# Low parts of the input projections' weights: an adding transfer onto the negated high parts in place of a VectorE subtraction

## The chip, the cores and the metric

The kernel runs on one core of one Trainium2 chip. The metric is the device time of one execution in microseconds (us). The kernel before took 2382.75 us as the median of 3 runs (2381.59 to 2386.46). The execution whose profile is read here took 2386.67 us; its trace spans 2384.9 us.

The engines are named as the profile names them: PE is TensorE (PEld its weight loads), DVE is VectorE, ACT is ScalarE, POOL is GpSimd, SP is SyncE. Each runs its own instructions strictly in the order in which they were recorded.

## The reference

The reference is a trunk of two layers on 1024 tokens of width 1024, in float32. Each layer is a mixer and then a convolutional feed-forward network (FFN), each between two RMS norms:

```python
for l in range(DEPTH):
    h = rms_norm(x, norm_mix_pre[l])
    proj = h @ w_in[l]                       # 1024 x 3072, twelve slices of 256 columns
    (c_a, c_gate, sb_q, sb_k, sb_v, r_q, r_k, r_v, r_g,
     sc_b, sc_c, sc_h) = jnp.split(proj, N_IN_SLICES, axis=-1)
    y_conf = conformer_conv(c_a, c_gate, ...)             # depthwise convolution of 31 taps
    y_sb = merge_heads(stick_breaking_attention(...))     # 4 heads, blocks of 128 queries
    y_ret = retention_mixer(r_q, r_k, r_v, r_g, ...)      # chunks of 128 tokens
    y_sc = short_gated_conv(sc_b, sc_c, sc_h, ...)        # 3 taps
    mix = jnp.concatenate([y_conf, y_sb, y_ret, y_sc], axis=-1) @ w_out[l]
    x = x + rms_norm(mix, norm_mix_post[l])
    f = conv_ffn(rms_norm(x, norm_ffn_pre[l]), ffn_up[l], ffn_conv_w[l], ffn_down[l])
    x = x + rms_norm(f, norm_ffn_post[l])
```

## The kernel before, in words

**Split products.** Every matrix product is done with both operands split into a high part (the value rounded to the type that PE multiplies) and a low part (what the rounding left). One product is three matmuls: high by high, high by low, low by high. For the input projection `hH` and `hL` are the parts of the normed tokens, kept in place, and `wh` and `wl` those of the weights.

**Weights of the input projection.** The 3072 columns of `w_in` are 24 weights of 1024 x 128 a layer. `load_weight` (L188 to L196) makes each one ready: SP issues the load of 512 KB into `wr`, of which there is one buffer; ACT casts it to `wh` (L193); the engine that is named in the queue, here always DVE, subtracts `wh` from `wr` into `wl` (L195). There are two buffers of `wh` and two of `wl`, so a weight can be made ready while PE works with the one before; PE frees the pair of the weight before that by its last matmul. `wr` is free for the next load when the last engine that reads it has done so.

**Projection.** `project` (L214) runs 48 matmuls of 128 x 512 for a weight (L210), in eight steps of six: two with `wh` and `hH`, two with `wh` and `hL`, two with `wl` and `hH`. The first matmul that needs `wl` is therefore the fifth. The first two weights of a layer are done together in `project_pair`.

**What runs between.** From the third weight on, PE's order is written out by hand (`manual_schedule`). Between two of the eight steps `run_slot` sets the other work of the mixer at slots of a fixed table. Three pieces of it matter here.

- Stick-breaking attention, in units: PE makes scores (L361, L362, L364) in one fixed bank of PSUM; ACT takes |z|, exp and log (L371 to L373); DVE combines (L375) and scans (L379); ACT takes an exp (L381); PE transposes (L396), ACT and DVE split the result (L181, L182), PE multiplies by the values (L409), and ACT and DVE (L416 to L418) add the parts. The next unit's scores wait until the scan has read the bank.
- Retention: PE makes products within chunks (L494) and outputs (L513, L518) in PSUM banks that it takes over from projections and from earlier steps; DVE must have drained these first (L182, L329, L379, L522, L523). Its norm takes a mean, a square and a variance (L530, L538 on PE; L541 and L542 on ACT; L543 and L546 on DVE). Its queries and keys are rotated on DVE (L437 to L439), with a swap of partitions by DMA between.
- The depthwise convolution: 30 taps for each of two halves, each tap one DVE instruction over about 1024 columns (L261). Taps have the lowest priority: the scheduler, which orders DVE, ACT, SP and POOL by its own estimates of time and by priorities, puts them wherever it thinks that DVE would be free.

**After the projections** come the output projection (its weights go through the same `wr`, L613), a boundary with the norms, and the FFN. In the FFN and for the first weights of a layer nothing is changed here.

Of the kernel before, what the change touches and what calls it, by code (L numbers as in the profile page):

```python
# [7 lines left out]
F32 = mybir.dt.float32  # L8
F32R = mybir.dt.float32r
AF = mybir.ActivationFunctionType  # L10
ALU = mybir.AluOpType
# [56 lines left out]
OTHER = (0, 2, 4)  # L68
HPR = 1000
HPW = 0  # L70
WPOOL = []
UPOOL = ()
SKEW = 0
NPLAIN = 3
# [12 lines left out]
def trunk_kernel(ctx, tc, x, w_in, w_out, w_up, w_down, params, gains, consts, rope, out):  # L87
    nc = tc.nc
# [32 lines left out]
    def ufree(*ts):  # L121
        for t in ts:
            free.append(slot_of.pop(id(t))[0])
# [60 lines left out]
    def gain(i):  # L184
        g = ualloc()
        nc.sync.dma_start(g, gains[i].partition_broadcast(P))
        return g

    def load_weight(src, eng):
        raw = wp.tile([P, KT, P], F32, tag="wr", name="wr", bufs=WR)  # L190
        nc.sync.dma_start(raw, src)
        wh = wp.tile([P, KT, P], F32R, tag="wh", name="wh")
        nc.scalar.copy(wh, raw)  # L193
        wl = wp.tile([P, KT, P], F32R, tag="wl", name="wl")
        eng.tensor_sub(wl, raw, wh.bitcast(F32))  # L195
        return wh, wl  # L196

    queue = []
    ready = []

    def prefetch(n=1):
        while queue and len(ready) < n:
            with tc.high_priority(offset=HPW):
                ready.append(load_weight(*queue.pop(0)))
# [345 lines left out]

    psum("pp")
    nc.scalar.preload_act_table_set("natural_log_exp_and_others")
    queue += [(w_in[0, n], nc.gpsimd if n in WPOOL else nc.vector) for n in range(24)]
    hhs = []
    for t in range(NB + SKEW):
        if t == XP:
# [22 lines left out]
    for l in range(DEPTH):  # L579
# [409 lines left out]
        def down_tok(gs, ws, t, first, final):  # L989
            ps = ptile(t % FB if final else nextp())  # L990
            down_mm(ps, gs, ws, t, range(2))
            if first:
                facc[t] = ualloc()
                with tc.high_priority(offset=HPE):
                    nc.vector.tensor_copy(facc[t], ps)
            else:
                nc.vector.tensor_add(facc[t], facc[t], ps)  # L997
            if final:
                boundary(t, facc[t], ps, g_post, g_pre, xin, xs[2 * l + 1] if g_pre is not None else out, XF[t])

        def down_end(gs, ws, t):

            rows = slice(t * P, (t + 1) * P)
            f, ps, xt = facc[t], ptile(t % FB), ualloc()
            nc.sync.dma_start(xt, xin[rows, :])
            tt = ualloc()
            ss = []
            for half in range(2):
                hs = slice(half * 512, (half + 1) * 512)
                down_mm(ps, gs, ws, t, (half,))  # L1010
                nc.vector.tensor_add(f[:, hs], f[:, hs], ps[:, hs])
                ss.append(square_sum(f[:, hs], ps[:, hs]))
                nc.vector.tensor_mul(tt[:, hs], f[:, hs], g_post[:, hs])
            nc.vector.tensor_add(ss[1], ss[0], ss[1])
            r = rstd_of(ss[1])
            for half in range(2):
                hs = slice(half * 512, (half + 1) * 512)
                nc.vector.scalar_tensor_tensor(tt[:, hs], tt[:, hs], r, xt[:, hs], ALU.mult, ALU.add)
                nc.sync.dma_start(out[rows, hs], tt[:, hs])
            ufree(xt, tt, f)  # L1020

        def down_load(j, where):

            w = down_split(w_down[l, j * P:(j + 1) * P, :], where)
            g = down_split(gd[j], None if where is None else where + 1)
            return g, w
# [37 lines left out]
        for ci, ch in enumerate(chunks):  # L1064
            final = ci == len(chunks) - 1
            if final:
                if not last:
                    queue += [(w_in[l + 1, n], nc.gpsimd if n in WPOOL else nc.vector) for n in range(24)]
                    prefetch(2)
                g_post, g_pre = gain(4 * l + 3), None if last else gain(4 * l + 4)  # L1070
            pairs = [loads[j] for j in ch]
            gs, ws = [p[0] for p in pairs], [p[1] for p in pairs]
            for t in range(NB):
                if final and last and t == NB - 1:
                    down_end(gs, ws, t)
                else:
                    down_tok(gs, ws, t, ci == 0, final)
                if t in (0, 1) and ci and todo and not final:
                    j, where = todo.pop(0)
                    loads[j] = down_load(j, where)  # L1080
            if places[ci] is None:
                for g, w in zip(gs, ws):
                    ufree(*g, *w)
            if ci == 0:
                for _ in range(4):
                    j, where = todo.pop(0)
                    loads[j] = down_load(j, where)
# [74 lines left out]
```

## Time and profile before

| | |
|---|---|
| median of 3 runs | 2382.75 us |
| the profiled execution | 2386.67 us |
| its span | 2384.9 us |
| PE busy | 2297.3 us (96%) |
| DVE busy | 1674.2 us (70%) |
| ACT busy | 1080.7 us (45%) |
| POOL busy | 196.5 us (8%) |

The page and the answers of the trace give times from the start of the span. Layer 0's mixer with its projections lies at about 25 to 430 us, layer 1's at about 1210 to 1640 us; the FFNs lie between and behind. A row of the timeline gives start, length, engine, line and operation, what it writes and reads, how many instructions are in the row, and in brackets how long the engine was idle before it and who released it.

### The profile page before, as it was taken

What the parts mean: (1) busy time and instruction counts of PE and PEld (TensorE: products, weight loads), DVE (VectorE), ACT (ScalarE), POOL (GpSimd) and SP (SyncE); (2) the same over time, 40 slices, a digit from 0 to 9 for tenths busy, and PEclk for the clock granted to TensorE, in tenths of its full rate; (3) what the DMA queues carried; (4) which work ended last, traced back from release to release, by engine and by line L of the source; (5) the groups of instructions that cost most, each with busy time, mean ns of one, the idle gap of its engine ahead of it and who ended that gap; (6) DMA issues with size and microseconds to landing.
All of it is one profiled execution on the core that took longest, in us unless ns stands there. A gap on an engine that the chain in (4) does not pass through costs nothing.

```text
span 2384.9 us, 26334 instructions
## 1 busy us (share of the span) xinstructions
PE 2297.3 (96%) x10596; PEld 1885.0 (79%) x10596; DVE 1674.2 (70%) x1749; ACT 1080.7 (45%) x1463; POOL 196.5 (8%) x84
## 2 busy tenths in 40 slices
PE   7998999999999999999999989999999999999998
PEld 6876787787888888788778767877888888888886
DVE  4699877559777777644556998775598777774445
ACT  5663565434455445421246535654344554453112
POOL 0000000000000000643210000000000000016420
PEclk9998999999999999999999989999999999999999
DMA  4212212412122224522222122123122222235223
GB/s 150 71 53 63 62 36 88 138 48 92 68 88 89 80 80 143 183 80 98 80 80 71 53 62 62 36 95 135 53 89 80 80 80 89 87 121 176 84 71 124
DMA packets 58810, 209.87 MB, mean 88 GB/s; under 512 B 7104, under 2 KB 7872, under 8 KB 58688
## 3 DMA queue, kind: packets, MB, share of 16 engines
q1 hardware_dynamic: 58688, 208.19, 26.7%
q8 instruction: 83, 1.36, 0.2%
q14 instruction: 39, 0.32, 0.0%
HBM read 159.93 MB, written 39.85 MB: 84 GB/s over the span
## 4 chain that ended last, share of the span: by engine, by line
PE 38%; DVE 7%; ACT 3%; DMA 1%; issue 1%; DVEq 0%; SPq 0%
PE pp L984 10%; PE pp L210 9%; PE ppx L901 8%; PE ppy L901 4%; DVE u L261 2%; PE ppz L901 2%; PE pp L738 1%; DVE u L182 1%; ACT u L151 1%; DMA wr<-in_w_out 1%; PE op L409 1%; DVE u L379 1%; DVE u L167 1%; PE tp L396 0%; DMA wr<-in_w_up 0%
## 5 line engine op out<-in xcount | busy, mean ns | idle before, releaser
L261 DVE SCALAR_TENSOR_TENSOR u<-u,par,u 128x1023 f32<-128x1023 f32 (+10 forms) x280 | 356.3, 1284 | 28.6 <-ACT u L793 24.4
L210 PE MATMUL pp<-hH,wh 128*128 128x512 f32 x960 | 327.2, 411 | 1.0 <-DVE u L182 0.5
L997 DVE TENSOR_TENSOR u<-u,pp 128x1024 f32<-128x1024 f32 x143 | 174.6, 1221 | 209.9 <-PE pp L984 209.8
L210 PE MATMUL pp<-hL,wh 128*128 128x512 f32 x960 | 312.7, 396 | 0.0
L210 PE MATMUL pp<-hH,wl 128*128 128x512 f32 x960 | 311.5, 395 | 0.0
L984 PE MATMUL pp<-u,u 128*128 128x512 f32 x1152 | 266.0, 392 | 6.1 <-ACT u L955 4.6
L984 PEld LDWEIGHTS pp<-u,u 128*128 128x128 f32 x1152 | 216.6, 189 | 52.4 <-ACT u L955 5.4
L974 POOL TENSOR_TENSOR hH<-u,hH 128x1024 fp32r<-128x1024 f32 x24 | 58.1, 2451 | 1946.5 <-ACT hH L973 1946.5
L210 PEld LDWEIGHTS pp<-hL,wh 128*128 128x128 f32 x960 | 183.6, 191 | 40.4
L210 PEld LDWEIGHTS pp<-hH,wl 128*128 128x128 f32 x960 | 183.2, 191 | 40.3
L210 PEld LDWEIGHTS pp<-hH,wh 128*128 128x128 f32 x960 | 172.6, 193 | 37.5 <-issue 5.9
L738 PE MATMUL pp<-u,hH 128*128 128x512 f32 x512 | 140.2, 392 | 0.4 <-ACT u L181 0.4
L984 PE MATMUL pp<-hH 128*128 128x512 f32 x576 | 131.5, 389 | 0.0
L984 PEld LDWEIGHTS pp<-hH 128*128 128x128 f32 x576 | 108.1, 188 | 22.4
L901 PE MATMUL ppx<-u,wh 128*128 128x512 f32 x384 | 118.4, 389 | 0.3 <-ACT u L926 0.3
L793 ACT ACTIVATE u<-u,par 128x1024 f32<-128x1024 f32 x76 | 87.8, 1156 | 67.4 <-DVE u L947 65.6
L738 PEld LDWEIGHTS pp<-u,hH 128*128 128x128 f32 x512 | 95.0, 188 | 20.4 <-ACT u L181 1.2
L195 DVE TENSOR_TENSOR wl<-wr,wh 128x1024 fp32r<-128x1024 f32 x60 | 73.3, 1221 | 50.9 <-ACT wh L193 50.7
L973 ACT CAST u<-u 128x1024 fp32r<-128x1024 f32 x48 | 50.2, 1052 | 128.9 <-DMA u<-in_w_down 85.7
L901 PE MATMUL ppx<-u,hH 128*128 128x512 f32 x352 | 108.4, 389 | 0.0
L193 ACT CAST wh<-wr 128x1024 fp32r<-128x1024 f32 x60 | 63.0, 1051 | 71.3 <-PE pp L210 57.1
L379 DVE TENSOR_TENSOR_SCAN u<-pp,u 128x1023 f32<-128x1023 f32 (+3 forms) x64 | 87.8, 1403 | 0.7
(240 smaller groups left out, 4400.3 us busy)
## 6 DMA issues: line engine op xcount, KB each, us to landing
wr<-in_w_up SPq DMA_DIRECT2D x50, 512.0 KB, 3.5
wr<-in_w_in SPq DMA_DIRECT2D x48, 512.0 KB, 3.5
gd<-u SPq DMA_DIRECT2D x44, 512.0 KB, 2.9
u<-in_w_down SPq DMA_DIRECT2D x44, 512.0 KB, 4.3
u<-gd SPq DMA_DIRECT2D x44, 512.0 KB, 3.9
u<-in_w_up SPq DMA_DIRECT2D x38, 512.0 KB, 4.3
xs<-u SPq DMA_DIRECT2D x24, 512.0 KB, 2.6
u<-xs SPq DMA_DIRECT2D x24, 512.0 KB, 3.4
```

Source lines behind the costliest of these rows:

```text
L193: nc.scalar.copy(wh, raw)
L195: eng.tensor_sub(wl, raw, wh.bitcast(F32))
L210: nc.tensor.matmul(ps[:, half * 512:(half + 1) * 512], w[:, kt, :], m[:, 4 * half:4 * half + 4, kt, :], start=(kt == 0 and m is hH and w i ...
L261: eng.scalar_tensor_tensor(acc[:, lo:hi], src[:, lo - s:hi - s], wc, acc[:, lo:hi], ALU.mult, ALU.add)
L379: nc.vector.tensor_tensor_scan(rev, z[:, o + 1:e + 1][:, ::-1], rev, r[:, e:e + 1], ALU.add, ALU.add)
L738: nc.tensor.matmul(ps[:, hs], a[:, t, k, :], w[:, hs], start=(k == 0 and a is hH and w is wo[k][0]), stop=(k == KT - 1 and a is hL))
L793: nc.scalar.activation(acc, ps, AF.Copy, scale=par[:, w + 2:w + 3])
L901: nc.tensor.matmul(ps, a[:, kt, :], x(m, kt), start=start and kt == 0 and a is wh and m == 0, stop=kt == 3 and a is wl, skip_group_check=True)
L973: nc.scalar.copy(h, raw)
L974: (nc.gpsimd if len(loads) >= 4 else nc.vector).tensor_sub(lo, raw, h.bitcast(F32))
L984: nc.tensor.matmul(ps[:, hs], a[:, ts_], w[:, hs], start=(i == 0 and w is h and a is gh), stop=(i == len(gs) - 1 and a is gl))
L997: nc.vector.tensor_add(facc[t], facc[t], ps)
```

## The change

For all weights of the input projection but the first two of each layer (44 in all), the engine of the subtraction becomes `None`. Then ACT, behind its cast to `wh`, writes the weight a second time, times -1, into `wl`; rounded to the same type, that is the negated high part. POOL then issues a transfer that reads the weight from DRAM again and adds it to what stands in `wl`, which leaves weight minus high part there. DVE has no part in it.

```diff
-WPOOL = []
...
         wl = wp.tile([P, KT, P], F32R, tag="wl", name="wl")
-        eng.tensor_sub(wl, raw, wh.bitcast(F32))
+        if eng is not None:
+            eng.tensor_sub(wl, raw, wh.bitcast(F32))
+            return wh, wl
+
+        nc.scalar.activation(wl, raw, AF.Copy, scale=-1.0)
+        nc.gpsimd.dma_start(wl, src, accum_op=ALU.add)
         return wh, wl
...
-    queue += [(w_in[0, n], nc.gpsimd if n in WPOOL else nc.vector) for n in range(24)]
+    queue += [(w_in[0, n], None if n >= 2 else nc.vector) for n in range(24)]
...
-                    queue += [(w_in[l + 1, n], nc.gpsimd if n in WPOOL else nc.vector) for n in range(24)]
+                    queue += [(w_in[l + 1, n], None if n >= 2 else nc.vector) for n in range(24)]
```

In the changed kernel the second write by ACT is L198 and the adding transfer L199; lines behind these are four higher than before (L375 is L379, L379 is L383), lines ahead of them one lower (L193 is L192).

PE's order is the same in both kernels. DVE's and ACT's are not, and the two layers are changed alike. Three places follow; names with numbers (u, pp) are buffers of SBUF and PSUM.

First, ACT at the start of layer 0's projections, before: the cast of the third weight, the two halves of the first keys (drained from PSUM), the two halves of the first queries, the cast of the fourth weight.

```order
L193 CAST wh<-wr 128x1024
L181 CAST u_18_396<-pp_6_292 64x1024
L181 CAST u_20_402<-pp_6_292 64x1024
L328 ACTIVATE u_22_408<-pp_7_293 64x1024
L328 ACTIVATE u_23_409<-pp_7_293 64x1024
L193 CAST wh<-wr 128x1024
```

The same place now:

```order
L192 CAST wh<-wr 128x1024
L198 ACTIVATE wl<-wr 128x1024
L180 CAST u_18_397<-pp_6_292 64x1024
L180 CAST u_20_403<-pp_6_292 64x1024
L192 CAST wh<-wr 128x1024
L332 ACTIVATE u_22_409<-pp_7_293 64x1024
L198 ACTIVATE wl<-wr 128x1024
L332 ACTIVATE u_23_410<-pp_7_293 64x1024
```

The second write of the third weight stands ahead of the keys, and the fourth weight's cast and second write have moved in among the queries.

Second, DVE in the retention stretch, before: outputs of retention (L522, L523), taps (L261), and between L375 and L379 of one attention unit the subtraction for a weight.

```order
L522 TENSOR_TENSOR u_95_1653<-pp_34_1792,u_95_1653 64x512
L261 SCALAR_TENSOR_TENSOR u_54_975<-u_53_971,par,u_54_975 128x1004
L523 TENSOR_TENSOR u_95_1653<-pp_34_1792,u_95_1653 64x512
L261 SCALAR_TENSOR_TENSOR u_54_975<-u_53_971,par,u_54_975 128x1003
L375 SCALAR_TENSOR_TENSOR u_105_1814<-pp_35_1804,u_104_1810 128x1024
L195 TENSOR_TENSOR wl<-wr,wh 128x1024
L379 SCALAR_TENSOR_TENSOR u_105_1814<-pp_35_1804,u_105_1814 128x1023
```

The same place now:

```order
L526 TENSOR_TENSOR u_95_1665<-pp_34_1805,u_95_1665 64x512
L265 SCALAR_TENSOR_TENSOR u_54_981<-u_53_977,par,u_54_981 128x997
L527 TENSOR_TENSOR u_95_1665<-pp_34_1805,u_95_1665 64x512
L265 SCALAR_TENSOR_TENSOR u_54_981<-u_53_977,par,u_54_981 128x996
L379 SCALAR_TENSOR_TENSOR u_105_1827<-pp_35_1817,u_104_1823 128x1024
L265 SCALAR_TENSOR_TENSOR u_54_981<-u_53_977,par,u_54_981 128x995
L383 SCALAR_TENSOR_TENSOR u_105_1827<-pp_35_1817,u_105_1827 128x1023
```

A tap stands where the subtraction stood, and the taps are eight further on (the last column counts down by one with each tap). From the L379 of the sixth attention unit (at about 120 us) to the one shown here, DVE had 47 taps and 8 subtractions; it now has 55 taps and none.

Third, the retention norm and the attention unit next to it. ACT before:

```order
L193 CAST wh<-wr 128x1024
L432 COPY u_117_1991<-pp_37_1854 128x1024
L541 ACTIVATE u_116_1965<-var,eps_t 128x512 x2
L542 ACTIVATE u_116_1965<-u_116_1965 128x1024
L371 ACTIVATE u_119_2019<-pp_40_2010 128x1024
```

ACT now:

```order
L192 CAST wh<-wr 128x1024
L436 COPY u_117_2005<-pp_37_1867 128x1024
L545 ACTIVATE u_116_1979<-var,eps_t 128x512 x2
L198 ACTIVATE wl<-wr 128x1024
L546 ACTIVATE u_116_1979<-u_116_1979 128x1024
L375 ACTIVATE u_119_2033<-pp_40_2024 128x1024
```

DVE there before:

```order
L375 SCALAR_TENSOR_TENSOR u_120_2023<-pp_40_2010,u_119_2019 128x1024
L379 SCALAR_TENSOR_TENSOR u_120_2023<-pp_40_2010,u_120_2023 128x255
L379 SCALAR_TENSOR_TENSOR u_120_2023<-pp_40_2010,u_120_2023 128x767
L438 TENSOR_TENSOR u_118_1993<-u_118_1993,u_109_1852 128x1024
L439 TENSOR_TENSOR u_108_1850<-u_108_1850,u_118_1993 128x1024
```

DVE there now:

```order
L379 SCALAR_TENSOR_TENSOR u_120_2037<-pp_40_2024,u_119_2033 128x1024
L442 TENSOR_TENSOR u_118_2007<-u_118_2007,u_109_1865 128x1024
L383 SCALAR_TENSOR_TENSOR u_120_2037<-pp_40_2024,u_120_2037 128x255
L383 SCALAR_TENSOR_TENSOR u_120_2037<-pp_40_2024,u_120_2037 128x767
L443 TENSOR_TENSOR u_108_1863<-u_108_1863,u_118_2007 128x1024
```

ACT's second write now stands ahead of the norm and of this attention unit, and on DVE a product of the rotation has moved ahead of the unit's two scans. POOL's order gains the 22 transfers of a layer as one block, ahead of its first other work in layer 0 and behind the last boundary of the FFN in layer 1.

## Rows read from the trace of the kernel before

**Rows 1.** The page, part 1: busy us of each engine, share, instructions.
```profile
PE 2297.3 (96%) x10596; PEld 1885.0 (79%) x10596; DVE 1674.2 (70%) x1749; ACT 1080.7 (45%) x1463; POOL 196.5 (8%) x84
```

**Rows 2.** The page, part 5: busy us, mean ns of one, idle before, releaser.
```profile
L261 DVE SCALAR_TENSOR_TENSOR u<-u,par,u 128x1023 f32<-128x1023 f32 (+10 forms) x280 | 356.3, 1284 | 28.6 <-ACT u L793 24.4
...
L793 ACT ACTIVATE u<-u,par 128x1024 f32<-128x1024 f32 x76 | 87.8, 1156 | 67.4 <-DVE u L947 65.6
...
L195 DVE TENSOR_TENSOR wl<-wr,wh 128x1024 fp32r<-128x1024 f32 x60 | 73.3, 1221 | 50.9 <-ACT wh L193 50.7
...
L193 ACT CAST wh<-wr 128x1024 fp32r<-128x1024 f32 x60 | 63.0, 1051 | 71.3 <-PE pp L210 57.1
```

**Rows 3.** Waits of PE, whole span: us in total, times, longest.
```profile
PE pp L513 <- DVE u L379: 8.6, 2, 4.3
PE pp L513 <- DVE u L329: 7.5, 2, 3.8
...
PE pp L513 <- DVE u L523: 4.9, 2, 3.0
...
PE pp L494 <- DVE u L182: 4.4, 2, 2.2
```

**Rows 4.** Timeline of DVE, retention stretch of layer 0.
```profile
243.92 1.23 DVE L195 TENSOR_TENSOR wl<-wr,wh 128x1024 fp32r<-128x1024 f32 x1 [1.08 <-ACT wh L193]
245.06 2.34 DVE L379 TENSOR_TENSOR_SCAN u<-pp,u 128x1023 f32<-128x1023 f32 x1
```

**Rows 5.** PE by 4 us: stretch, length, busy, clock, DMA share, GB/s.
```profile
204.00:208.00 4.00, 1.94 (x9) 1.00 0.61 133
208.00:212.00 4.00, 3.87 (x29) 0.64 0.75 160
212.00:216.00 4.00, 4.00 (x24) 0.93 0.26 104
```

**Rows 6.** Timelines of ACT, DVE and PE, start of layer 0's projections.
```profile
42.90 1.06 ACT L193 CAST wh<-wr 128x1024 fp32r<-128x1024 f32 x1 [9.12 <-PE pp L210]
...
47.42 1.23 DVE L182 TENSOR_TENSOR u<-pp,u 64x1024 fp32r<-64x1024 f32 x1 [1.08 <-ACT u L181]
...
48.79 0.70 PE L210 MATMUL pp<-hH,wh 128*128 128x512 f32 x2 [0.27 <-DVE u L182]
...
49.80 0.62 PE L210 MATMUL pp<-hH,wl 128*128 128x512 f32 x2
```

**Rows 7.** Page, part 6: DMA issues, KB each, us to landing.
```profile
wr<-in_w_in SPq DMA_DIRECT2D x48, 512.0 KB, 3.5
```

**Rows 8.** Timelines of ACT and PE: weight nine, before and at its use.
```profile
129.03 1.06 ACT L373 ACTIVATE u<-u 128x1024 f32<-128x1024 f32 x1
...
139.99 0.62 PE L210 MATMUL pp<-hH,wl 128*128 128x512 f32 x2
```

**Rows 9.** Timelines of ACT, DVE and PE, retention norm of layer 0.
```profile
271.73 1.27 ACT L541 ACTIVATE u<-var,eps_t 128x512 f32<-128x512 f32 x2
273.03 1.06 ACT L542 ACTIVATE u<-u 128x1024 f32<-128x1024 f32 x1
...
276.95 1.07 ACT L373 ACTIVATE u<-u 128x1024 f32<-128x1024 f32 x1
...
278.05 1.23 DVE L375 SCALAR_TENSOR_TENSOR u<-pp,u 128x1024 f32<-128x1024 f32 x1 [0.15 <-ACT u L373]
279.31 2.45 DVE L379 TENSOR_TENSOR_SCAN u<-pp,u 128x255 f32<-128x255 f32 x2
281.68 1.20 DVE L438 TENSOR_TENSOR u<-u,u 128x1024 f32<-128x1024 f32 x1
...
281.82 0.44 PE L361 MATMUL pp<-u,u 128*128 128x384 f32 x1
```

**Rows 10.** Timelines of DVE and PE, key transposes of layer 0.
```profile
338.90 1.29 DVE L182 TENSOR_TENSOR u<-tp,u 128x512 fp32r<-128x512 f32 x2 [1.18 <-ACT u L181]
...
339.64 1.25 PE L450 MATMUL tp<-ident,u 128*128 128x128 f32 x8 [0.55 <-DVE u L182]
```

## The prediction

> **What bounds the kernel now.** I read the page's busy shares first. PE is busy 96% of the span, DVE 70%, ACT 45%, POOL 8% [rows 1]: PE is the bound, and an edit counts only by what it does to the 88 us in which PE is idle and to PE's clock. Next the waits of PE. In the mixers its long waits are for DVE: PSUM banks that DVE drains late (L513 and L494), two waits of each kind, one a layer, 8.6, 7.5, 4.9 and 4.4 us in all [rows 3], so 25.4 us, or 12.7 a layer. In that stretch DVE runs back to back, and the subtraction stands right in front of a scan on which PE waits [rows 4]. Last PE's clock by slices of 4 us: after the L494 wait, which leaves 1.94 us of work in the slice 204 to 208, the next slices are granted 0.64 and 0.93 of the full 2.4 GHz, a mixture with the lower level of 1.2 [rows 5]; that costs (0.36 + 0.07) x 4 = 1.7 us more. A reader should take two things from this: PE has time to win near DVE's backlog, and a new wait of about 2 us can cost a dip of the clock as well.
>
> **What the change removes.** 44 subtractions of 1.22 us, 53.8 us of DVE. DVE also stood idle 50.7 us in front of L195 until ACT had cast `wh` [rows 2]; for these 44 that goes too. But what PE waits for is decided by what stands in DVE's order between two such waits, and the scheduler fills the holes with taps. From the L379 near 120 us to the one that releases PE at 247 us, 8 subtractions go out and 8 taps come in. A tap takes 1.284 us and a subtraction 1.221 [rows 2], so this is 8 x 0.063 = +0.5 us. One of the 8 was waited for: DVE idled 1.08 us at 243.92 for the cast [rows 4], and a tap needs none. Together -0.6 us a layer where 53.8 us of freed DVE could suggest much more. The taps that moved forward are missing behind that place, where PE has no long wait to lose. Between the dense stretch and the end of the mixer the freed DVE time meets no wait of PE.
>
> **What it adds on ACT.** 44 second writes. The operation isn't in the trace. The cast of the same tile takes 1051 ns; an ACTIVATE of this size with a factor per partition takes 1156 [rows 2]; I take 1.06, as the plain ACTIVATE L542 [rows 9], 46.6 us in all. Most of it lies in ACT's idle time. In each layer three of the writes stand in a chain on which PE waits with no slack:
>
> 1. Start of the projections. ACT casts the third weight from 42.90 and then drains the first keys; DVE follows, its second L182 ends at 48.65, and PE starts the third project at 48.79, after 0.27 us of waiting for it [rows 6]. The second write now stands between cast and keys: +1.06. DVE's subtraction goes: it could start at the cast's end, 43.96, and took 1.22, to 45.2, while ACT had the first half of the keys done a cast's length after 43.96, by 45.0; this gives back 0.2. Net +0.9.
> 2. Retention norm. L541, L542, an attention unit's L371 to L373, L375 and the scans run back to back, and the scans end at 281.76, 0.06 us before PE's L361 [rows 9]. The second write moves behind L541: +1.06. On DVE L438 (1.20) now stands between L375 and the scans: +1.20, less the 0.06. So +2.2 us, a new wait.
> 3. Key transposes. PE waits 0.55 us at 339.64 for L182, which itself waits 1.18 for ACT [rows 10]. A second write now stands in ACT's chain to that L182, and an earlier one has pushed the unit before: +1.06 for the one on the path, and I take nothing for the other. So +1.1.
>
> A layer thus gains 0.9 + 2.2 + 1.1 - 0.6 = +3.6 us, two layers +7.2. Of the clock: wait 2 is new and at 2.2 us as long as the L494 wait, so I add one dip of 1.7 a layer [rows 5], +3.4. The bounds of this are none (0) and two dips a layer (+6.8, if wait 3 also gets one).
>
> **What it adds in transfers.** `wl` now is ready when ACT's second write, POOL's issue and a transfer of 512 KB are through. The nearest row is SP's load of the same bytes, 3.5 us from issue to landing [rows 7]. From below: a little under 3.5 is not excluded. From above: it reads both the weight and what stands in `wl`, and the load of the next weight is released by the same write, so twice the row, 7.0. The tightest place is the third weight. Its second write ends at 43.96 + 1.06 = 45.0; the first matmul with `wl` is at 49.80 [rows 6], and with 0.9 from point 1 at 50.7. That is 5.7 us of room: 3.5 costs nothing, 7.0 costs 1.3 a layer. I take the middle, 5.25, which is hidden. Elsewhere there is more room; a tight one is the ninth weight, whose second write follows the L373 that ends at 130.09 and whose `wl` is wanted at 139.99 [rows 8]: 9.9 - 1.06 = 8.8 us. POOL runs nothing else in the mixers, and its transfers wait only for ACT, so nothing is queued behind them that anyone waits for; in layer 1 they stand behind POOL's boundary work, which is over when they are wanted. On SP, loads of weights move past swaps and copies of keys; since a load waits for ACT's write, some of these start 1 to 2 us later, with more slack than that. The 22 MB (44 x 512 KB) more that are read come over the same 16 DMA engines, which the slices show 0.26 to 0.75 busy where the mixer is densest [rows 5]; I take nothing for it.
>
> The rows say nothing on the price of the addition. By the Trainium skill (Collectives: The Full Stack, section "The bandwidth ceiling: the fold count and why AG ≠ RS ≠ AR") a reducing transfer isn't slowed by its adder but because it reads two sources, which halves its rate. An estimate by that page doubles the row's transfer, at most 7.0 us, and the sum would be +2.6 us for the two layers; no run so far shows it.
>
> **Sum.** 7.2 + 3.4 = +10.6 us. Against the profiled execution that is 2386.67 + 10.6 = 2397.3, its span 2395.5 with 1.8 outside. That execution lies 3.9 above the median, and what the change adds is the same for either: 2382.75 + 10.6 = 2393.3 us.
>
> **The rivals.**
> A. DVE's relief reaches PE. If the taps that come in are not on the path (DVE gets ahead where I think it is full), the 8 subtractions are 8 x 1.22 = 9.8 us of the 12.7 that PE waits in that stretch. It decides from the point where the freed time passes the 4.2 us a layer of the three ACT terms. Two layers: 2 x (4.2 - 9.8) = -11.2, or 2371.6 without a change of clock. For it: DVE really is back to back there, and those waits are the longest in the mixers. Against it: the order puts a tap in place of the subtraction in front of the very scan that PE waits for.
> B. The transfer is slow. At 10 us from issue to landing the third weight makes PE wait 10 - 5.7 = 4.3 us, the ninth 10 - 8.8 = 1.2, and I allow 2.5 for the rest: 8 a layer, with the other terms 2393.3 + 16 = 2409. For it: accumulating and POOL's issue are both unseen here. Against it: from 3.5 to 8 us it costs next to nothing.
> C. Nothing to measure. The slack that I read at one instant is larger (PE waits elsewhere a bit longer, so that points 2 and 3 have room), no dip follows, and +3.6 or less remains, against a gain of the same size: 2382 to 2387.
>
> The Trainium skill has a rule that speaks against the change (SBUF — State Buffer, section "Who interferes with whom"): descriptors of POOL's transfers are written through a port that DVE shuts while it runs in its two-port mode. What DVE runs there is taps and subtractions with two inputs from SBUF, which by the same page only close the read side; so by it B gets no more than I give it below.
>
> **How the numbers follow.** Chances: forecast 0.50, A 0.17, B 0.17, C 0.16. A measurement of this kernel can tell about 0.2%, 4.8 us, from no change. The forecast's own range runs from 2387 (no dip, wait 2 halved) to 2402 (two dips a layer, a third weight that waits); of its 0.50 I give 0.45 to slower and 0.05 to same. A gives 0.14 faster and 0.03 same. B is slower, 0.17. C gives 0.14 same, 0.01 each way. Together faster 0.15, same 0.22, slower 0.63. The range of 8 in 10 takes in C and most of B and leaves out most of A: 2379 to 2410.
>
> **What would show it.** In the profile after: DVE busy down by some 54 us and ACT up by some 47; PE's waits for L379 at L361 some 2 us longer in each layer near 282 us and at the same place of layer 1, with a slice of lower clock behind; the start of the third project some 0.9 us later after its weights; the L513 waits much as before, in sum within 2 us a layer. PE must not wait for the adding transfer at L210; if it does, B is right and the third weight shows it first. If the L513 waits have shrunk to a few us in all, A is right and my count of taps was the wrong step.

## The result, and the profile after

The changed kernel takes 2406.1 us in the median of four runs (2401.66 to 2408.07), the kernel before 2384.6 beside it: a ratio of 1.0089, 95% interval 1.0068 to 1.0109. It is slower by 21.5 us; forecast were 10.6. The profiled execution has a span of 2402.4 us against 2384.9, 17.5 more, and those can be followed instruction by instruction; the other 4.0 are that the profiled execution of before lies 2.1 us above its median here and that of the changed kernel 1.9 below.

The page, part 1 (busy us, share of the span, instructions), answers to [rows 1]:

```profile
PE 2305.0 (96%) x10596; PEld 1890.6 (79%) x10596; DVE 1624.3 (68%) x1705; ACT 1121.0 (47%) x1507; POOL 234.6 (10%) x128
```

DVE has lost 49.9 us and ACT has gained 40.3, in time that counts the short overlap of neighbouring rows once; forecast were some 54 and 47. PE is busy 7.7 us longer (2297.3 before) on the same 10596 instructions, most of that in matmuls at the lower clock; the other 9.8 of the 17.5 us are waits. For the clock 3.4 were forecast. The second write is a group of its own in the lines on the tile `wl` (duration in ns min/median/max, first and last start); its 1.058 us is what the prediction took. The last line, from issue to landing, is that of the adding transfer, L199:

```profile
L198 ACT ACTIVATE wl<-wr x44: 1042/1058/1068, 43.7 to 1596.5; 128x1024 fp32r<-128x1024 f32 x44
L199 POOL DMA_DIRECT2D wl<-in_w_in x44: 856/865/1007, 45.1 to 1597.9; - x44
DMA to landing us min/median/max: 5.9/6.9/8.7
```

PE's waits over the whole span (us in total, times, longest) answer to [rows 3]; L513 is now L517, L494 is L498, L361 is L365, L210 is L214, L379 is L383, L329 is L333, L523 is L527:

```profile
PE pp L365 <- DVE u L383: 12.4, 8, 2.6
PE pp L517 <- DVE u L527: 7.4, 2, 4.5
PE pp L498 <- DVE u L181: 6.1, 2, 3.0
PE pp L517 <- DVE u L383: 5.8, 2, 3.1
...
PE pp L214 <- DMA wl<-in_w_in: 5.6, 2, 3.3
...
PE pp L517 <- DVE u L333: 4.2, 2, 2.9
```

One line is new: PE waits twice, once a layer, for an adding transfer. The L517 waits came to 17.4 us (21.0 before), the L498 wait to 6.1 (4.4). Of the old waits those for a scan at L365 have grown most; before they were:

```profile
PE pp L361 <- DVE u L379: 7.3, 6, 1.7
```

PE issues the same instructions in the same order in both kernels, so the start of one and the same matmul in the two traces says by how much the changed kernel is late there. This table is worked out from the two timelines (all in us):

```
stretch, and the matmul at its end      before    after   late by   made here   forecast
third weight's projection starts         48.79    49.38     0.59       0.6         0.9
its first matmul with wl                 49.80    53.84     4.04       3.4         0
2 us of work later                       52.09    57.73     5.64       1.6         0
op of the unit ahead of the norm        267.70   273.22     5.52      -0.1        -0.6
scores behind the norm (L361)           281.82   289.08     7.26       1.7         2.2
a projection behind it                  284.57   293.35     8.78       1.5         1.7
key transposes (L450)                   339.64   349.44     9.80       1.0         1.1
layer 1's projections begin            1218.66  1226.29     7.63      -2.2         0
third weight and what follows          1240.48  1252.66    12.18       4.6         0.9
op of the unit ahead of the norm       1458.46  1471.57    13.11       0.9        -0.6
scores behind the norm, and clock      1475.78  1492.21    16.43       3.3         3.9
key transposes                         1530.32  1547.79    17.47       1.0         1.1
```

The start, by the timelines of ACT, POOL, DVE and PE (start, duration, instruction, idle before and its releaser), answers to [rows 6]:

```profile
43.73 1.06 ACT L198 ACTIVATE wl<-wr 128x1024 fp32r<-128x1024 f32 x1
...
45.11 1.01 POOL L199 DMA_DIRECT2D wl<-in_w_in  x1 [44.66 <-ACT wl L198]
...
48.01 1.23 DVE L181 TENSOR_TENSOR u<-pp,u 64x1024 fp32r<-64x1024 f32 x1 [1.07 <-ACT u L180]
...
49.38 0.70 PE L214 MATMUL pp<-hH,wh 128*128 128x512 f32 x2 [0.97 <-DVE u L181]
...
53.84 0.73 PE L214 MATMUL pp<-hH,wl 128*128 128x512 f32 x2 [3.30 <-DMA wl<-in_w_in]
```

ACT's write ends at 44.79 (forecast: 45.0). POOL issues 0.3 us later, and the data land 8.7 us behind that, at 53.8, when `wl` has been wanted since 50.5. In layer 1 the third weight's transfer takes 7.7 us and PE waits 2.3. PE's clock behind the wait, in slices of 4 us (stretch, length, busy, granted clock, DMA share, GB/s):

```profile
48.00:52.00 4.00, 1.56 (x6) 1.00 1.04 236
52.00:56.00 4.00, 2.16 (x6) 0.81 1.00 201
56.00:60.00 4.00, 4.00 (x15) 0.76 0.92 209
...
288.00:292.00 4.00, 2.92 (x11) 0.75 0.01 4
292.00:296.00 4.00, 4.00 (x20) 0.82 0.00 0
```

The DMA engines are full (share 1.0) while the adding transfer runs: the next weight's load and the key swaps run beside it. After the wait the clock is a mixture of 2.4 and 1.2 GHz for two slices, (0.19 + 0.24) x 4 = 1.7 us. The last two rows are the dip behind the retention norm, (0.25 + 0.18) x 4 = 1.7.

The norm by its timelines answers to [rows 9]:

```profile
278.32 1.07 ACT L198 ACTIVATE wl<-wr 128x1024 fp32r<-128x1024 f32 x1
...
279.27 1.06 ACT L546 ACTIVATE u<-u 128x1024 f32<-128x1024 f32 x1
...
284.30 1.23 DVE L379 SCALAR_TENSOR_TENSOR u<-pp,u 128x1024 f32<-128x1024 f32 x1 [0.19 <-ACT u L377]
...
285.44 1.22 DVE L442 TENSOR_TENSOR u<-u,u 128x1024 f32<-128x1024 f32 x1
...
286.57 2.45 DVE L383 TENSOR_TENSOR_SCAN u<-pp,u 128x255 f32<-128x255 f32 x2
...
289.08 0.44 PE L365 MATMUL pp<-u,u 128*128 128x384 f32 x1 [1.77 <-DVE u L383]
```

L198 stands in the chain that ends in L379, and L442 (L438 before) between L379 and the scans: both as forecast, and PE's wait is 1.77 us where it was under 0.1.

### The profile page after: what moved, and what is told of

It reads as the page before. It is cut to its first block, busy times and chain, and to the rows that moved or that the text cites. A ratio compares the mean times of both kernels' runs of the same rounds, so it can differ in the third digit from the quotient of the medians.

```text
span 2402.4 us, 26411 instructions
## 1 busy us (share of the span) xinstructions
PE 2305.0 (96%) x10596; PEld 1890.6 (79%) x10596; DVE 1624.3 (68%) x1705; ACT 1121.0 (47%) x1507; POOL 234.6 (10%) x128
## 4 chain that ended last, share of the span: by engine, by line
PE 35%; DVE 9%; ACT 3%; DMA 2%; issue 1%; DVEq 0%; SPq 0%; ACTq 0%
PE pp L988 10%; PE pp L214 8%; PE ppx L905 7%; PE ppy L905 4%; DVE u L265 3%; PE ppz L905 2%; DVE u L181 1%; PE pp L742 1%; DVE u L383 1%; ACT u L150 1%; DMA wr<-in_w_out 1%; DVE u L166 1%; DMA wr<-in_w_up 0%; DVE u L253 0%; DVE u L379 0%
## 5 line engine op out<-in xcount | busy, mean ns | idle before, releaser
L265 DVE SCALAR_TENSOR_TENSOR u<-u,par,u 128x1023 f32<-128x1023 f32 (+11 forms) x280 | 357.8, 1284 | 29.3 <-ACT u L797 24.4
L214 PE MATMUL pp<-hH,wh 128*128 128x512 f32 x960 | 329.0, 414 | 2.1 <-DVE u L181 2.0
L214 PE MATMUL pp<-hH,wl 128*128 128x512 f32 x960 | 312.9, 397 | 5.6 <-DMA wl<-in_w_in 5.6
L214 PE MATMUL pp<-hL,wh 128*128 128x512 f32 x960 | 314.9, 399 | 0.0
L214 PEld LDWEIGHTS pp<-hH,wl 128*128 128x128 f32 x960 | 184.6, 192 | 47.1 <-DMA wl<-in_w_in 6.4
L214 PEld LDWEIGHTS pp<-hL,wh 128*128 128x128 f32 x960 | 184.7, 192 | 40.8
L214 PEld LDWEIGHTS pp<-hH,wh 128*128 128x128 f32 x960 | 173.5, 194 | 38.9 <-issue 5.2
L199 POOL DMA_DIRECT2D wl<-in_w_in x44 | 38.2, 868 | 737.9 <-ACT wl L198 672.4
L192 ACT CAST wh<-wr 128x1024 fp32r<-128x1024 f32 x60 | 63.0, 1050 | 92.0 <-PE pp L214 78.8
L181 DVE TENSOR_TENSOR u<-tp,u 128x512 fp32r<-128x512 f32 x96 | 62.5, 684 | 48.6 <-ACT u L180 48.4
```

Source lines behind the costliest of these rows:

```text
L181: nc.vector.tensor_sub(l, src, h.bitcast(F32))
L199: nc.gpsimd.dma_start(wl, src, accum_op=ALU.add)
L214: nc.tensor.matmul(ps[:, half * 512:(half + 1) * 512], w[:, kt, :], m[:, 4 * half:4 * half + 4, kt, :], start=(kt == 0 and m is hH and w i ...
L265: eng.scalar_tensor_tensor(acc[:, lo:hi], src[:, lo - s:hi - s], wc, acc[:, lo:hi], ALU.mult, ALU.add)
```

## The experiments

Each was timed against runs of the kernel before on the same chip.

**The third weight kept on DVE.**

```
-  None if n >= 2 else nc.vector
+  None if n >= 3 else nc.vector
```

> The third weight of each layer (n = 2) keeps its subtraction on DVE; the other 42 stay changed. Theory T (the price at the start of the projections is the adding transfer of that one weight: PE waits 3.3 and 2.3 us for it, and the clock falls behind each wait for 1.6 and 1.7 us more): 2406 - 9 = 2397 us, PE waits 0 for a transfer at L214, and the fourth weight is not late. Rival R (the transfer is too slow as such, so the wait moves on to the fourth weight, or the DMA traffic of the others is what costs): 2403 or more, with a wait for wl of 2 us or more at the fourth weight.

Measured: 2394.2 us, ratio 1.0046 [1.0029, 1.0064]; the changed kernel had 1.0089, so this one weight costs some 10 us, 0.43% of 2385, to about 6 us either way by the two intervals. Theory T holds in its size. In one point it failed: the fourth weight is late. Waits of PE of this kernel:

```profile
PE pp L214 <- DMA wl<-in_w_in: 1.7, 2, 1.5
```

In layer 0 PE reaches the fourth weight 6.4 us earlier than in the changed kernel (61.2 against 67.5), and POOL issues its transfer 3.0 us later (54.98 against 51.99): its load now starts behind the key swaps, at 48.5, where it started ahead of them at 44.8. So PE waits 1.5 us for it.

**Without the adding transfer.**

```
-        nc.gpsimd.dma_start(wl, src, accum_op=ALU.add)
```

> The adding transfer is left out and everything else of the change kept: ACT's second write stays, and the projections use the negated high part itself as wl (the low parts are not made). Theory T (of the 21 us some 10 are the transfer at two places, the rest is ACT's second write and DVE's order): 2406 - 10 = 2396 us, with PE's waits for L383, L181 and at L454 as in the changed kernel. Rival R (22 MB more on the DMA engines slow the loads, the key swaps and the rest all along): 2390 or less.

Measured: 2394.9 us, 1.0038 [1.0024, 1.0053]. This kernel leaves the low parts of the 44 weights out. As T: all transfers together cost, within the intervals, what the third weight's costs (12 and 10 us), and the 22 MB of traffic cost nothing else that shows (the next kernel has the traffic and takes the same time). The rest, some 9 us over before, is ACT's second write with DVE's order.

**A plain transfer instead of an adding one.**

```
-        nc.gpsimd.dma_start(wl, src, accum_op=ALU.add)
+        nc.gpsimd.dma_start(wl, src)
```

> The changed kernel with a plain transfer from the same queue in the place of the adding one: it overwrites the negated high part with the weight itself (so wl is the weight and not its low part). Theory Add (the adding transfer takes 6.9 us because it reads two sources): about 4 us from issue to landing, as SP's load of the same bytes, no wait for wl at the third weight or under 1 us, and 2396 us as without a transfer. Rival Queue (POOL's issue and its queue cost, whatever the transfer does): 6 us or more from issue to landing, waits as in the changed kernel, 2402 us or more.

Measured: 2394.0 us, 1.0043 [1.0029, 1.0057], and no wait for `wl`. Here `wl` is the whole weight and not its low part. Issue to landing (part 6 of its page: KB each, median us):

```profile
wr<-in_w_in SPq DMA_DIRECT2D x48, 512.0 KB, 3.6
wl<-in_w_in POOLq DMA_DIRECT2D x44, 512.0 KB, 4.6
```

Theory Add: on the same queue the addition makes 4.6 into 6.9 us, and at the third and fourth weights 5.2 into 8.6 in layer 0 and 5.4 into 7.8 in layer 1. Of this 0.3 is POOL's own instruction (0.87 against 0.53 us). POOL's queue itself adds only 1.0 to SP's 3.6. Part 3 of the pages (packets, MB, share of the time of 16 engines) has the queue of the 44 transfers, first adding, then plain:

```profile
q0 software_dynamic: 6336, 23.07, 5.2%
...
q0 software_dynamic: 6336, 23.07, 2.9%
```

The same packets and bytes hold the DMA engines 1.8 times as long. The Trainium skill (Collectives: The Full Stack, section "The bandwidth ceiling: the fold count and why AG ≠ RS ≠ AR") has the reduce step of a collective at half the rate of a copy, since it reads two sources. The direction agrees, and the time on the DMA engines comes near it with 5.2 / 2.9 = 1.8. From issue to landing the factor is only 6.9 / 4.6 = 1.5 in the median, and 1.65 and 1.45 at the third and fourth weights of the two layers. That it is the second source which costs, and not the adding itself, no run here separates.

**No low parts at all.**

```
+        if eng is None:
+            return wh, StandIn()      # every [:, kt, :] is the tile identr
```

> For the 44 weights neither subtraction, nor second write, nor transfer: PE multiplies by a fixed 128 x 128 tile in the place of wl (the low parts are left out). This is the most that freeing DVE can give. Theory T (the freed 54 us of DVE are filled with taps that stand before the same scans, so PE gets little of it): 2381 to 2386 us, within 4 us of before, and the ACT terms gone (no second write before the retention norm at 282 us and before the key transposes at 340 us). Rival A (DVE's relief does reach PE, and only ACT's second write and the transfer hide it): 2376 us or less.

Measured: 2387.4 us, 1.0015 [1.0003, 1.0026]. This kernel leaves the low parts out as well. Freed of 54 us of work on DVE, with nothing added anywhere, the kernel was a little slower than before, just outside what theory T allowed and far from A. Timelines near the end of layer 0's projections show why, first of DVE before, then of DVE and PE in this kernel (L497 before is L502 here):

```profile
367.77 1.23 DVE L195 TENSOR_TENSOR wl<-wr,wh 128x1024 fp32r<-128x1024 f32 x1
...
369.35 1.23 DVE L497 TENSOR_TENSOR u<-pp,tri 128x1024 f32<-128x1024 f32 x1
```

```profile
371.20 1.23 DVE L181 TENSOR_TENSOR u<-wr,u 128x1024 fp32r<-128x1024 f32 x1 [3.38 <-ACT u L180]
372.34 1.22 DVE L502 TENSOR_TENSOR u<-pp,tri 128x1024 f32<-128x1024 f32 x1
...
373.62 2.61 PE L499 MATMUL pp<-u,u 64*128 64x128 f32 x22 [2.76 <-DVE u L502]
```

A subtraction stood ahead of the mask's product (L502) and is gone; the scheduler now puts the split of an output weight (L181) there, which waits 3.38 us for ACT and so for a load. L502, for which PE waits, stands behind it. By the starts of the same matmuls this costs 5.7 us in layer 0 and 6.1 in layer 1, clock included.

**The same with that order kept.**

```
-  None if n >= 2 else nc.vector
+  nc.vector if n in (0, 1, 22) else None
```

> The kernel without low parts (PE multiplies by a fixed tile in the place of wl), but the subtraction of n = 22 is kept on DVE, and with it the order near 371 us: the mask's product L502 again stands ahead of the output weight's split L181, as before, and not behind it. Theory T (without that swap freeing DVE is worth some 9 us; the swap made PE wait 2.7 us for L502 and lowered the clock, 5.7 and 6.1 us in the two layers): 2387.4 - 11.5 = 2376 us. Rival (freeing DVE is worth nothing wherever the order is mended, the wait comes back elsewhere): 2383 us or more.

Measured: 2377.6 us, 0.9972 [0.9961, 0.9983]. As T. So the freed DVE is worth some 7 us, 0.28%, when nothing is added elsewhere, and a single swap in the order had hidden it.

**The subtraction on POOL.**

```
-WPOOL = []
+WPOOL = list(range(2, 24))
```

> The kernel before with the subtraction of the 44 weights on POOL instead of DVE; no second write, no adding transfer. A POOL pass over two inputs of this size took 2.45 us (L978) against DVE's 1.22. Theory T (taps fill DVE as in the changed kernel, ACT is untouched, POOL is 1.2 us later with each wl, which has that room): within 6 us of the kernel without low parts, 2380 to 2390 us. Rival P (POOL and DVE disturb each other in SBUF: taps longer than 1.284 us beside POOL's 108 us, or POOL's pass much longer than 2.45 beside DVE's taps): 2400 us or more.

Measured: 2397.5 us, 1.0058 [1.0043, 1.0073]: between the two, nearer to P. Its mechanism is there. The rows are taps beside POOL's subtraction, and the taps as a group (busy, mean ns):

```profile
226.04 4.59 DVE L261 SCALAR_TENSOR_TENSOR u<-u,par,u 128x1007 f32<-128x1007 f32 x2
226.30 3.27 POOL L195 TENSOR_TENSOR wl<-wr,wh 128x1024 fp32r<-128x1024 f32 x1 [16.93 <-ACT wh L193]
```

```profile
L261 DVE SCALAR_TENSOR_TENSOR u<-u,par,u 128x1023 f32<-128x1023 f32 (+11 forms) x280 | 374.1, 1347 | 29.1 <-ACT u L793 24.4 <-ACT u L268 0.8
```

Two taps take 4.59 us instead of 2.57, and the 280 taps 374.1 against 356.3 [rows 2]. How much of the time lost comes from this and how much from the new order was not separated.

**One weight back, at the retention norm.**

```
-  None if n >= 2 else nc.vector
+  nc.vector if n in (0, 1, 16) else None
```

> The changed kernel with the one weight n = 16 kept on DVE, whose second write stood in front of the retention norm (near 282 us). Theory T (that second write and the order that came with it made PE wait 1.7 us more at L365 and lowered its clock for 1.5 us more, in each layer): 2406 - 6.5 = 2399.5 us, PE's wait at L365 near 289 us gone. Rival (the wait is made by DVE's L438, which stays ahead of the scans, or comes back at the next scan): 2403 us or more.

Measured: 2395.9 us, 1.0055 [1.0034, 1.0076]: some 8 us less than the changed kernel (to about 7 either way), and the interval takes in the 6.5. By the starts of the same matmuls the norm's stretch is 3.3 us shorter in layer 0 and 3.4 in layer 1; the rest of what its profiled execution gains lies mostly in layer 1 ahead of the norm, where waits and clock changed too. The scans come first again:

```profile
282.93 2.45 DVE L383 TENSOR_TENSOR_SCAN u<-pp,u 128x255 f32<-128x255 f32 x2
...
285.30 1.20 DVE L442 TENSOR_TENSOR u<-u,u 128x1024 f32<-128x1024 f32 x1
...
285.43 0.44 PE L365 MATMUL pp<-u,u 128*128 128x384 f32 x1
```

The second write and DVE's swap both went at once, so their shares are read from the timelines and not from a run.

**Seven weights back, and the two halves of that.** Each keeps n = 0 and 1 on DVE as well:

```
e6:  n in (2, 3, 8, 12, 13, 16, 20)
e8:  n in (2, 3, 16, 20)
e9:  n in (2, 3, 8, 12, 13)
```

> Kept on DVE: the weights whose second write or transfer stood in a chain to PE (n = 2 and 3 at the start, 8 before the scan near 142 us, 12 and 13 before the keys' transposes and the retention's scores, 16 before the retention norm, 20 before the key transposes at 340 us). The other 30 stay changed. Theory T (the loss is made at these places and nowhere else): 2406 - 10 (start) - 2 (fourth weight) - 6.6 (norm with its dips) - 2 (keys) - 3 (scan at 142 us with its dips) = 2382 us, no slower than before. Rival R (every kind of order that the scheduler finds with some subtractions gone puts taps before scans that PE waits for): 2390 us or more, with new waits for L383 or L333.

> Kept on DVE: n = 2 and 3 (start), 16 (retention norm), 20 (key transposes). Theory Sum (each place has its own price and the prices add): 2394 with the third weight kept, less 3 for the fourth's wait of 1.5 us and its dip, less 6.6 for the norm, less 2 for the keys: 2382 us. Rival Order (the better part of what the kernel with nine on DVE gained comes from n = 8, 12 and 13, which decide how the taps fall before the scores and scans between 140 and 250 us): 2388 us or more.

> Kept on DVE: n = 2 and 3 (start), 8, 12 and 13, but not 16 and 20. Theory Sum: the norm and the keys' transposes cost 8.6 us more than in the kernel with nine on DVE, 2374.5 + 8.6 = 2383 us. Rival Order: these three decide the order, and most of the gain stays: 2379 us or less.

Measured: e6 2374.5 us, 0.9961 [0.9948, 0.9973]; e8 2383.8, 1.0005 [0.9993, 1.0018]; e9 2384.0, 1.0004 [0.9993, 1.0014]. The halves agree with theory Sum, within the intervals (both keep the fourth weight, so that its small part counts in each). Against the kernel with the third weight kept (1.0046), e8 takes off 0.41% and e9 0.42%, and e6 lies another 0.44% and 0.43% below them. The seven together gain more than theory T said (2382), and e6 is faster than both kernels. Waits of PE of e6:

```profile
PE pp L517 <- DVE u L333: 8.2, 2, 4.3
PE pp L517 <- DVE u L383: 8.2, 2, 4.1
PE pp L365 <- DVE u L383: 7.3, 6, 1.7
...
PE pp L498 <- DVE u L181: 2.9, 2, 2.2
PE pp L517 <- DVE u L527: 1.3, 2, 0.9
```

Against [rows 3], the waits for L523 (4.9) and L494 (4.4) have shrunk to 1.3 and 2.9. The larger part of the gain is not in the waits:

```profile
PE 2289.4 (96%) x10596; PEld 1879.6 (79%) x10596; DVE 1639.2 (69%) x1719; ACT 1107.0 (47%) x1493; POOL 221.5 (9%) x114
```

The span of its profile is 12.4 us under before, and 7.9 of these are PE's busy time (2297.3 in [rows 1]) on the same instructions, most of it less time at the lower clock. By the starts of the same matmuls 3.0 of the 12.4 lie between the two mixers, where nothing was changed.

## Why the prediction was right, and where its size was off

Slower was the likeliest outcome forecast, and 2406.1 lies in the range of 8 in 10, 2379 to 2410. But it is above the forecast's own range, 2387 to 2402 (whose upper end is also more than its terms add up to: 2382.75 + 7.2 + 6.8 + 2.6 = 2399.4), and nearer to rival B's 2409 than to 2393.3. The outer range held because it was drawn to take in B, and in one place B is what happened. The sum of 10.6 us was half of the 21.5 measured.

1. **The transfer (forecast: hidden).** This is the mis-sized term. "I take the middle, 5.25, which is hidden" stood on SP's load of 3.5 us; the adding transfer took 6.9 in the median and 8.7 and 7.7 at the third weight of the two layers, above the upper end of 7.0. The room was right, 5.7 us forecast and 5.7 there (44.8 to 50.5). PE waited 3.3 and 2.3 us, and behind each wait the clock fell, for which the sum had nothing. In all the start cost 5.6 and 4.6 us where 0.9 was forecast, +8.4; the first two experiments put 10 to 12 us on it. So the forecast met rival B at the one place that B named first; the ninth weight did not wait. Of B's two reasons the adding took the time; POOL's issues took 0.86 to 1.01 us each. What the argument overlooked is that the DMA engines are full at the third weight: the key swaps and the next load run just then, and 8.7 us is the longest landing of the 44. That the crowding made it so long is argued and not tested, since a landing of 8.1 us at 85 us came at a share of 0.74. "I take nothing for it" fits the mixer as a whole, where no other weight was late; there it may not.
2. **The drain of the keys (+0.9).** Measured +0.6 in layer 0 and, by PE's wait there, +0.7 in layer 1.
3. **Retention norm (+2.2, and a dip of 1.7).** Right: +1.7 and +1.5 in layer 0, 3.3 in layer 1, through both instructions that were named; with the weight put back the same stretches are 6.7 us shorter, where the traces had given 6.6.
4. **Key transposes (+1.1).** Right: +1.0 in each layer.
5. **DVE's count (-0.6 a layer).** Measured -0.1 and +0.9, so this term was wrong by 2.0 us in all. At the 247 us for which the count was made, layer 0 was 1.5 us later than at the end of its start. Near 140 us a tap now stands between L379 and the scans too, a place that was not looked at; PE starts L365 1.1 us later for it, and the clock that falls behind the wait costs 1.5 more, of which the next wait gives back 0.4. DVE's timelines there, before and in the changed kernel:

```profile
131.46 1.22 DVE L375 SCALAR_TENSOR_TENSOR u<-pp,u 128x1024 f32<-128x1024 f32 x1
132.71 0.29 DVE L417 TENSOR_TENSOR u<-op,u 64x128 f32<-64x128 f32 x1
133.03 2.46 DVE L379 TENSOR_TENSOR_SCAN u<-pp,u 128x127 f32<-128x127 f32 x2
```

```profile
137.42 1.22 DVE L379 SCALAR_TENSOR_TENSOR u<-pp,u 128x1024 f32<-128x1024 f32 x1
138.55 1.27 DVE L265 SCALAR_TENSOR_TENSOR u<-u,par,u 128x1013 f32<-128x1013 f32 x1
139.73 2.45 DVE L383 TENSOR_TENSOR_SCAN u<-pp,u 128x127 f32<-128x127 f32 x2
```

   Behind 247 us, where PE had now waited 2.7 us and not 4.3, a higher clock gave 1.6 back. That the net of layer 0 comes near the forecast is luck: its parts are not those that were counted.
6. **Rival A.** With the order kept and nothing added, DVE's relief was worth 7 us, with nine weights on DVE 9 (0.39%), not the 2 x 9.8 that A put on it, but more than the 1.2 of the count in the sum. In the changed kernel second writes and transfer outweigh it: relief alone is 0.9972 of before (in a kernel that keeps one of the 22 subtractions a layer), with the second writes as well 1.0038 (some 16 us more), with the transfers too 1.0089 (some 12 more), each step to some 4 to 6 us. The sum had 11.8 us for the second writes with their dips, and nothing for the transfers.
7. Between the layers the changed kernel gains 2.2 us, which no step explains. Most of that stretch is the feed-forward part, which holds no changed instruction, and in the profiled executions of the other kernels it moved as well, by -4.2 us with the third weight kept and by -0.1 without the adding. Of the 2.2, 0.6 lie in a wait near 456 us and 1.0 at the start of layer 1's projections, where the profile before shows a granted clock of 0.57 (1216 to 1220) and the one after 1.00 (1224 to 1228). What moves the clock there is left open.

## What to carry to other kernels

An engine freed off the critical path gives what the new order gives: count, at each place where the bound engine waits without slack, which instruction now stands in front of the one it waits for. Moving work to a queue with latency pays only where there is room for its longest landing, so price the transfer by that and not by a median, let alone by that of a plain load. Such a change need not be made for all instances: leaving out the seven of 22 a layer with no room turned 0.9% slower into 0.4% faster.

## What the runs showed of the hardware

- An adding transfer of 512 KB took 5.9 to 8.7 us from issue to landing in the changed kernel, a plain one on the same queue 3.9 to 7.5, and POOL's issue 0.87 us against 0.53. The DMA engines were held 1.8 times as long by the adding ones (5.2% against 2.9%).
- A tap with two inputs from SBUF took up to 3.4 us beside a POOL subtraction, 1.28 alone; the POOL pass went up to 3.56 from 2.35. That agrees with the Trainium skill (SBUF — State Buffer, section "Who interferes with whom"), by which a DVE instruction with two inputs from SBUF contends with a GpSimd instruction that reads it.
- A wait of PE of 1.8 us (norm) was followed by as long a dip of the clock as one of 3.3 us (third weight): 1.7 us each.
